# Encoder layer on eight cores: scores of an attention visit ahead of the value products of two earlier visits, a second home for folded matrices, and a new seed for the plan

## The chip, the cores and the metric

The kernel runs on the 8 cores of one Trainium2 chip (two dies of four cores). Each core computes two of the 16 sequences, with no exchange between cores. The metric is the device time of the slowest core in microseconds (us).

Some executions fall into a second, slower state, in which the cores of a die have a lower granted clock, whatever the kernel. Of the first four executions of the kernel before, two took 2221 and 2222 us and two 2437 and 2497 us.

TensorE does the matmuls, ScalarE the exponentials and many copies, VectorE sums, normalisation and many copies. In the profile's names, ps is the accumulation memory of TensorE (8 banks of 128 x 512 f32: four for scores, four for the rest). M_p holds 2 KB and 4 KB tiles, W_p bf16 weights, KV_p keys and values, S_p small bf16 tiles. wst is the weights in f32 in main memory, wsc a scratch area there for weights converted or folded once and read again.

## The reference, cut to what matters

```python
n1 = rmsnorm(h, g_mix)
q, k, v, u, gates = split(n1 @ w_in)
q, k = apply_rope(rmsnorm(q)), apply_rope(rmsnorm(k))
a = gqa_block_attention(q, k, v) @ w_attn_up       # 2048 x 2048 scores for each of 8 heads
p = (pooled(u) @ pool_w * pool_scale) @ w_pool_up
h = h + (g_a * a + g_p * p) @ w_out
# cross-attention into 256 memory tokens
xk, xv = split(rmsnorm(mem) @ w_xkv)
h = h + softmax((rmsnorm(h) @ w_xq) @ xk.T) @ xv @ w_xo
h = h + square(relu(rmsnorm(h) @ w_ff1)) @ w_ff2
return rmsnorm(h)
```

The kernel folds the cross-attention's weights with the memory tokens once per sequence (w_xq with xk into tiles A0 and A1, xv with w_xo into tiles B), 16 tiles of 4 KB for the two sequences. These are the "folded matrices". They are made in the first 230 us, beside attention 0.

## The kernel before

The work of a core is written as a list of some 6350 operations. A planner gives each an engine, a place in that engine's order, and slots for its tiles; the program then contains exactly this order, with the semaphores that it needs. A core has eight attentions (two sequences, four tiles of 512 tokens). Each has 32 visits. A visit makes four banks of scores for 256 keys and two heads, takes the exponential of all four in one instruction of ScalarE, and its value products follow one or two visits later, two visits at a time:

```python
NV, PVB = 32, 2
def visit(k):
    mms, W = [], []
    pv = range(k - PVB, k) if k >= 1 and k <= NV and k % PVB == 0 else ()
    for kk in pv:                      # value products of the two preceding visits
        P = st_["P"].pop(kk)
        ...
        mms.append(mm(..., [(Vt, kt), P], mode="c", ...))
    if k < NV:
        S = [V("S", "E") for _ in range(4)]      # the four score banks
        W.extend(S)
        ...
        mms.append(mm(..., [(K, kt // 4), q], mode="r", ...))    # scores
    if mms:
        PE(mms, W)                     # ONE operation: products first, then scores
    if k < NV:
        P = V("P", "M2")               # probabilities: a 4 KB slot
        A(exponential of ps[:, 0:4, :] into P, 2048, ...)
```

The tiles live in pools of slots. Raw weights, probabilities, running sums and gates share the ten slots of M2; bf16 weights and folded matrices share the ten slots of W:

```python
SIZES = dict(W=(10, 2048, BF16), M2=(10, 1024, F32), M1=(32, 512, F32), S1=(52, 512, BF16), KV=(4, 2048, BF16))
SEED, JITTER = 10, 60.0                # priorities are perturbed by up to 60 ns
```

After planning, `keep_warm` puts matmuls of ones by ones, whose result nobody reads, into the gaps that the plan expects in TensorE's order, where TensorE would be busy less than 80% of 3.4 us:

```python
WARM_MIN, WARM_MARGIN, WARM_SPAN, WARM_SHARE = 500.0, 450.0, 3400.0, 0.8
...
room[g[0]] = int((g[2] - g[1] - WARM_MARGIN) / FILL)      # FILL = 216 ns
```

I call these **fillers**. In the profile they are `ps<-ones_bf`. L700 is the helper's line that all matmuls have in the kernel before (L723 after), L1165 the exponential (L1197), L720 and L723 the copies and casts by ScalarE and by VectorE or GpSimd (L743, L746), L808 the logarithm of the softmax's reciprocal (L831).

The softmax here doesn't subtract the row's maximum and nothing guards it: scores larger than these inputs give would overflow.

## Time and profile before

| | value | read as |
|---|---|---|
| fast runs | 2221.2 and 2222.4 us | slow runs 2437 and 2497 are left out |
| mean span of the eight cores in the profile | 2209.3 us | less uneven than the slowest core alone; from the first to the last busy instruction, so about 5 us less than the cores view, whose mean is 2214.4 |
| attention 0, first to last exponential | 135.2 us | the stage beside the folds |
| attention 4's first to attention 7's last exponential | 937.3 us | the late stage, full of matmuls |
| fillers | 219 | 90 before 40 us, 38 in the late stage |

The stage lengths are means over the eight cores of the profile, from the starts of the 256 exponentials (32 for each attention). The prediction shows the page's lines on the engines, the stages and the waits. Two rows of the groups by form of TensorE belong beside them (columns: line, engine, operation, tiles, shapes, count, then busy us and mean ns, then idle us of TensorE just before them and what ended it):

```profile
L700 PE MATMUL ps<-S_p,KV_p 64*128 64x512 bf16 x1024 | 155.5, 382 | 6.5 <-ACT M_p L1165 5.5 <-ACT M_p L801 0.4 <-DVE M_p L1314 0.3
L700 PE MATMUL ps<-M_p,KV_p 128*64 128x512 bf16 x1024 | 137.5, 388 | 8.6 <-ACT M_p L1165 6.2 <-DVE M_p L1372 0.9 <-DVE W_p L723 0.8
```

The first row is the scores, the second the value products: together they wait 5.5 + 6.2 = 11.7 us for the exponential (L1165).

### The profile page before, as it was taken

To read this page: it belongs to the slowest core of one execution; us is meant where nothing else is said; L and a number is where in the kernel's file an instruction comes from. 1 tells how busy PE (TensorE), PEld (TensorE's weight loads), DVE (VectorE), ACT (ScalarE), POOL (GpSimd) and SP (SyncE) were. 2 spreads that over 40 slices of the span, in tenths; PEclk is the share of its full clock that TensorE was granted. 3 is DMA by queue.
4 is the path that set the end of the run, shared out by engine and by line. 5 is a ranking of instruction groups with operands and counts; after the bars stand their busy time and mean duration, and the time that the engine had idled before them with its cause. 6 is when DMAs were issued, how large, how long until landed. Compare 5 with 4: busy or idle time off the path is not lost.

```text
span 2223.7 us, 34683 instructions; the slowest of 8 cores (2205.3 to 2223.7 us)
## 1 busy us (share of the span) xinstructions
PE 2168.1 (97%) x11354; PEld 954.4 (43%) x11354; DVE 1455.3 (65%) x1793; ACT 1492.3 (67%) x1905; POOL 392.8 (18%) x286
## 2 busy tenths in 40 slices
PE   9989999999999999999999999999999999999998
PEld 5443343444444444444434443444444443444457
DVE  6877786679765687756764588457764687456403
ACT  6877778668784577844787378845786478835551
POOL 1222331223122242121120122002110112000200
PEclk9999999999999999999999999999999999999999
DMA  9977968899596973945533462436433463336353
GB/s 287 311 217 221 317 215 274 278 308 321 172 305 206 301 248 115 321 141 186 185 113 124 150 213 91 146 132 204 157 114 124 155 214 109 128 130 221 126 168 133
DMA packets 143022, 438.27 MB, mean 197 GB/s; under 512 B 16000, under 2 KB 20224, under 8 KB 142848
## 3 DMA queue, kind: packets, MB, share of 16 engines
q1 hardware_dynamic: 142848, 436.06, 60.2%
q8 instruction: 96, 1.57, 0.3%
q14 instruction: 78, 0.64, 0.1%
HBM read 372.03 MB, written 63.96 MB: 196 GB/s over the span
## 4 chain that ended last, share of the span: by engine, by line
PE 87%; DMA 5%; ACT 3%; DVE 2%; issue 2%; SPq 0%; DVEq 0%; ACTq 0%; POOL 0%; POOLq 0%
PE ps L700 87%; DMA M_p<-wst 3%; ACT M_p L1165 1%; DMA wsc<-W_p 1%; DMA outT<-M_p 1%; ACT W_p L720 0%; DVE W_p L723 0%; DMA W_p<-wsc 0%; SPq L708 0%; DVE M_p L813 0%; ACT M_p L808 0%; DMA M_p<-xT 0%; DVE M_p L1281 0%; ACT M_p L787 0%; DVE M_p L1372 0%
## 5 line engine op out<-in xcount | busy, mean ns | idle before, releaser
L700 PE MATMUL ps<-S_p,W_p 128*128 128x512 bf16 (+1 forms) x6400 | 1367.9, 369 | 10.2 <-ACT M_p L808 4.3
L700 PEld LDWEIGHTS ps<-S_p,W_p 128*128 128x128 bf16 x6400 | 611.0, 98 | 734.3 <-issue 91.3
L1165 ACT ACTIVATE M_p<-ps 128x2048 bf16<-128x2048 f32 x256 | 479.4, 1873 | 225.8 <-PE ps L700 221.0
L700 PE MATMUL ps<-M_p,W_p 128*128 128x512 bf16 (+1 forms) x1608 | 369.5, 379 | 6.6 <-ACT M_p L808 2.5
L1176 DVE TENSOR_TENSOR M_p<-M_p 128x1024 f32<-128x1024 f32 x216 | 274.8, 1272 | 148.7 <-ACT M_p L1165 144.2
L1177 DVE TENSOR_TENSOR M_p<-M_p 128x1024 f32<-128x1024 f32 x216 | 305.0, 1412 | 17.0 <-DVE M_p L1176 1.8
L796 POOL TENSOR_TENSOR M_p<-M_p 128x512 f32<-128x512 f32 x70 | 107.4, 1535 | 779.0 <-ACT M_p L787 667.5
L700 PEld LDWEIGHTS ps<-M_p,W_p 128*128 128x128 bf16 x1608 | 153.7, 98 | 203.7 <-issue 28.4
L787 ACT ACTIVATE M_p<-M_p 128x512 f32<-128x512 f32 x216 | 134.0, 624 | 118.0 <-DVE M_p L1372 45.4
L723 POOL CAST W_p<-M_p 128x1024 bf16<-128x1024 f32 x89 | 109.3, 1237 | 480.5 <-PE ps L700 303.0
L1391 ACT ACTIVATE M_p<-ps 128x512 f32<-128x512 f32 x256 | 151.9, 594 | 52.2 <-PE ps L700 50.0
L700 PE MATMUL ps<-S_p,KV_p 64*128 64x512 bf16 x1024 | 155.5, 382 | 6.5 <-ACT M_p L1165 5.5
L1395 ACT ACTIVATE S_p<-M_p 128x512 bf16<-128x512 f32 x221 | 139.2, 630 | 20.5 <-ACT M_p L1391 0.7
L700 PE MATMUL ps<-M_p,KV_p 128*64 128x512 bf16 x1024 | 137.5, 388 | 8.6 <-ACT M_p L1165 6.2
L720 ACT ACTIVATE W_p<-M_p 128x1024 bf16<-128x1024 f32 x66 | 69.0, 1050 | 96.0 <-PE ps L700 84.2
L1243 ACT ACTIVATE M_p<-ps,nbg 128x512 f32<-128x512 f32 x128 | 86.9, 684 | 53.0 <-PE ps L700 52.2
L1407 DVE TENSOR_TENSOR M_p<-ps,M_p 128x512 f32<-128x512 f32 x56 | 38.7, 691 | 118.8 <-PE ps L700 118.8
L723 DVE CAST W_p<-M_p 128x1024 bf16<-128x1024 f32 x69 | 50.4, 742 | 59.6 <-DMA M_p<-wst 23.5
L700 PEld LDWEIGHTS ps<-M_p,KV_p 128*64 128x64 bf16 x1024 | 49.6, 110 | 86.4 <-issue 62.7
L700 PEld LDWEIGHTS ps<-S_p,KV_p 64*128 64x128 bf16 x1024 | 29.6, 94 | 112.6 <-issue 112.5
L700 PE MATMUL ps<-W_p,M_p 128*128 128x384 bf16 (+1 forms) x512 | 75.3, 299 | 1.5 <-ACT W_p L720 0.9
L1394 DVE TENSOR_TENSOR S_p<-ps,M_p 128x512 bf16<-128x512 f32 x35 | 24.1, 689 | 70.8 <-ACT M_p L1391 70.6
(87 smaller groups left out, 1780.1 us busy)
## 6 DMA issues: line engine op xcount, KB each, us to landing
W_p<-wsc SPq DMA_DIRECT2D x391, 512.0 KB, 4.4
M_p<-wst SPq DMA_DIRECT2D x228, 512.0 KB, 8.7
wsc<-W_p SPq DMA_DIRECT2D x69, 512.0 KB, 8.5
M_p<-xT SPq DMA_DIRECT2D x120, 256.0 KB, 8.8
outT<-M_p SPq DMA_DIRECT2D x56, 256.0 KB, 5.7
n1d<-M_p SPq DMA_DIRECT2D x28, 256.0 KB, 6.6
M_p<-n1d SPq DMA_DIRECT2D x28, 256.0 KB, 7.2
pdd<-M_p SPq DMA_DIRECT2D x14, 256.0 KB, 7.1
```

What stands on the lines that cost most here:

```text
L700: return e.matmul(out(), lhsT=lhsT(), rhs=rhs(), start=start, stop=stop, skip_group_check=True, **kw)
L720: return e.activation(out=dst(), in_=src(), func=AF.Copy)
L723: return e.tensor_copy(out=dst(), in_=src())
L787: A(lambda e: e.activation(out=ap(sq), in_=src(), func=AF.Square), 512, False, R, [sq])
L796: TT(lambda e: e.tensor_tensor(out=ap(out), in0=ap(acc), in1=ap(sq), op=ALU.add), [acc, sq], [out])
L1165: A(lambda e: e.activation(out=b16(P).rearrange("p (a n) -> p a n", n=512), in_=ps[:, 0:4, :], func=AF.Exp, scale=0.125), 2048, True, S, [P])
L1176: D(lambda e: e.tensor_tensor(out=ap(acc), in0=ap(acc), in1=lo(), op=ALU.add), 1024, [P, acc], [acc], port=True)
L1177: D(lambda e: e.tensor_tensor(out=ap(acc), in0=ap(acc), in1=hi(), op=ALU.add), 1024, [P, acc], [acc], port=True)
L1243: A(lambda e, b=b, i=i: e.activation(out=ap(Et)[:, i * 512:(i + 1) * 512], in_=ap(b), func=AF.Exp, bias=nbg[:, i * 8 + j:i * 8 + j + 1], s ...
L1391: A(lambda e: e.activation(out=ap(rl), in_=ap(b), func=AF.Relu), 512, True, [b], [rl])
L1395: e.activation(out=ap(H), in_=ap(rl), func=AF.Square))
L1407: D(lambda e: e.tensor_tensor(out=ap(t), in0=ap(b), in1=ap(r), op=ALU.mult), 512, [b, r], [t])
```

## The change

Its intent: the exponential of an even visit shouldn't have to wait for 0.99 us of value products that stand ahead of its scores; folded matrices shouldn't have to wait for a W slot; and the plan is made again with the best seed. The core of the diff:

```diff
-SEED, JITTER = 10, 60.0
+ELSEWHERE = ("A0", "A1", "B")
+SEED, JITTER = 33, 60.0
@@ the planner's loop
+        if glued is not None:            # the products follow their visit's scores at once
+            ...
+            best = (r, "pe", glued)
@@ V(name, pool)
+            if name in ELSEWHERE:
+                v.alt = "M2"
@@ visit(k)
-                    mms, W = [], []
+                    mms, W, late = [], [], []
@@
-                        W.extend(S)
+                        smm = []
@@
-                                mms.append(mm(lambda h=h, t=t: ap(S[2 * t + h]),
+                                smm.append(mm(lambda h=h, t=t: ap(S[2 * t + h]),
@@
-                    if mms:
+                        first = PE(smm, S + W)
+                        if mms:
+                            for P in late:
+                                G.wait(first, P)      # so that the products need not wait again
+                            first.glue = PE(mms, W)
+                    elif mms:
                         PE(mms, W)
```

The planner takes an M2 slot for a folded matrix only if that is free over 300 ns earlier than a W slot.

More of the change, by code (lines that the diff above doesn't have):

```diff
@@ L45, in O2, with GROUP @@
     return ch["up"] + ch["wo"] + ch["sc"] + ch["xo"]
+def GROUP(s, tb):
+    return 2
 def AUX(query, attention, tile, blocks):
@@ L98 @@
     __slots__ = ("i", "engs", "fn", "mms", "deps", "succ", "vals", "allocs", "vt", "U", "early", "ndep", "ready", "eng",
-                 "start", "finish", "dma", "extra", "modes", "dur", "order", "place", "ps", "key", "eng_store", "port", "lead")
+                 "start", "finish", "dma", "extra", "modes", "dur", "order", "place", "ps", "key", "eng_store", "port", "lead", "glue")
 class Graph:
@@ L117, in _keys, with wait @@
             yield from self.parts.get(k, (k,))
+    def wait(self, o, v):
+        for d in self.lw[(v, 0)]:
+            if d not in o.deps:
+                d.succ.append(o)
+            o.deps[d] = 0.0
     def op(self, engs, fn, R=(), W=(), early=1e12, mms=None, dma=None, vt=None, store=False, port=False):
@@ L126, in op @@
         o.ps = False
-        o.eng_store, o.port, o.lead = store, port, 0.0
+        o.eng_store, o.port, o.lead, o.glue = store, port, 0.0, None
         reads = [(k, 0.0) for k in self._keys(R)]
@@ L292, in alloc_time @@
         return t
+    glued = None
     while n_left:
@@ L298, in schedule @@
         best = None
-        for level in range(2):
+        if glued is not None:
+            r = free_at["pe"]
+            for d, off in glued.deps.items():
+                r = max(r, d.finish + latency(d.eng, "pe") - off)
+            assert glued.ndep == 0 and all(v.slot is not None for v in glued.allocs)
+            best = (r, "pe", glued)
+        for level in range(2 if best is None else 0):
             for e in engines:
@@ L348, in schedule @@
             cand[e2].remove((o.U, o.i, o))
+        glued = o.glue
         o.eng = e
@@ L657, in ap @@
                 return ps[:, 4 + v.slot, :]
-            return tens[v.pool][:, v.slot, :]
+            t = tens[v.pool][:, v.slot, :]
+            return t.bitcast(BF16) if v.pool == "M2" and v.name in ELSEWHERE else t
         def halves(name, n):
@@ L1097, in attention_steps @@
             K, Vt = kv_tiles(s)
-            NV, PVB = 32, 2
+            NV, PVB = 32, GROUP(s, tb)
             def visit(k):
                 def f():
-                    mms, W = [], []
+                    mms, W, late = [], [], []
                     finish = []
@@ L1107, in f @@
                         P = st_["P"].pop(kk)
+                        late.append(P)
                         if v == 0:
@@ L1129, in f @@
                             ac = st_["accb"][c]
+                            late.append(ac)
                             parts.append((lambda h, ac=ac: b16(ac)[:, h * 512:h * 512 + 512], ac))
@@ L1142, in f @@
                         ac = st_["accb"][c]
+                        late.append(ac)
                         for h in range(2):
```

## The prediction

> **What bounds the kernel now.** I read the page's busy table first, then the cores, then the windows by stage, and inside the one stage with idle TensorE the waits, the chain and the timeline.
>
> ```profile
> PE 2168.1 (97%) x11354; PEld 954.4 (43%) x11354; DVE 1455.3 (65%) x1793; ACT 1492.3 (67%) x1905; POOL 392.8 (18%) x286
> ```
> ```profile
> core 1: 2223.7 us, clock 0.996
> core 2: 2205.3 us, clock 0.998
> ```
> ```profile
> core 1: us, PE busy (x) PEld busy (x) DVE busy (x) ACT busy (x) POOL busy (x), PEclk, DMA share, GB/s
> ...
> 92.00:232.00 140.00, 120.86 (x685) 49.63 (x685) 103.68 (x116) 107.65 (x108) 26.74 (x22) 0.96 0.79 240
> 232.00:400.00 168.00, 164.78 (x817) 66.77 (x818) 126.28 (x149) 138.00 (x175) 48.19 (x36) 0.99 0.83 267
> 400.00:2212.00 1812.00, 1793.71 (x9278) 785.80 (x9277) 1155.03 (x1393) 1178.52 (x1488) 297.12 (x206) 1.00 0.55 183
> ```
>
> TensorE is busy 97% of the span, so only its idle time and its useless work can go. After 400 us it idles 1812 - 1793.7 = 18.3 us in 1812. The one weak stage is 92 to 232 us: 19.1 us idle of 140 and a granted clock of 0.96. That stage holds the folds of the memory matrices with the attention of block 0 beside them. Core 2 runs the same program, had a clock of 1.00 there, and is 18.4 us shorter: the slowest core is slow because of this stage.
>
> From the steps between starts of consecutive matmuls in the trace of core 1 I split its span: 2084 us of streaming, 63 us of array-mode switches (660 steps that are 95 ns longer, 311 ns where the usual step is 216), 66 us of waits (5 of them lost to the half clock), and about 10 us before the first and after the last matmul. The streaming includes 219 matmuls of ones by ones that the plan itself puts into expected gaps to keep the clock up: 219 x 0.216 = 47 us, 109 - 30 = 79 of them before 30 us, where nothing else can run. So 66 + 47 = 113 us is all that any plan could win with the same arithmetic, and some 20 us of it is the unavoidable start.
>
> What TensorE waits for in the weak stage (us in total, times, longest):
>
> ```profile
> PE ps L700 <- ACT M_p L1165: 7.2, 9, 1.6
> PE ps L700 <- ACT M_p L808: 4.3, 1, 4.3
> PE ps L700 <- DVE W_p L723: 3.7, 6, 1.1
> PE ps L700 <- ACT W_p L720: 2.8, 1, 2.8
> ```
>
> L1165 is the softmax exponential. The tile view of wsc and the chain, both from the weak stage, show who is behind the others:
>
> ```profile
>   ACT W_p L720: 10.5, 3
>   DVE W_p L723: 9.0, 2
> ```
> ```profile
> 156.19 8.00 DMA wsc<-W_p
> ...
> 217.56 14.38 DMA wsc<-W_p
> ```
>
> Evictions of folded matrices into W slots (L720, L723) sit 10.5 and 9.0 us waiting for a store of an earlier folded matrix to leave its slot, and those stores are 22.4 us of the chain of 140. The 4.3 us wait at 166 us comes right after the first of them.
>
> **What the skill says, and the trace.** "PSUM — Partial Sum Buffer", Terms: two engines on one bank at once is an error. The four score banks are all read by one exponential, so the next scores must wait for its end; in the trace scores start 0.14 us after it, never before. "ScalarE: Activation LUTs", What ACT_TABLE_LOAD costs: 186 ns plus 0.833 ns per element, 1.89 us for 2048; the trace has 1.873, so the exponential is at its floor and can only start sooner. "TensorEngine Tiling (Array Packing)", Key Properties: changing the tiling mode drains the array; the trace shows 95 ns per change. "TensorE: Matmul & The Clock Gate", What's actually happening: an idle window of about 3.4 us halves the clock; here the 12 matmuls of 256 columns after the 4.26 us gap took 2.53 us where twelve others took 1.48.
>
> **Part 1, scores first.** The loop of block 0 where nothing else fills it (start, us, what):
>
> ```profile
> 144.42 1.05 PE L700 MATMUL ps<-M_p,KV_p 128*64 128x512 bf16 x8 [0.76 <-ACT M_p L1165]
> 145.41 0.61 PE L700 MATMUL ps<-S_p,KV_p 64*128 64x512 bf16 x4
> 145.94 1.48 PE L700 MATMUL ps<-S_p,W_p 128*128 128x256 bf16 x12
> 148.19 0.61 PE L700 MATMUL ps<-S_p,KV_p 64*128 64x512 bf16 x4 [0.76 <-ACT M_p L1165]
> ```
> ```profile
> 146.17 1.88 ACT L1165 ACTIVATE M_p<-ps 128x2048 bf16<-128x2048 f32 x1 [0.42 <-PE ps L700]
> 148.95 1.88 ACT L1165 ACTIVATE M_p<-ps 128x2048 bf16<-128x2048 f32 x1
> ```
>
> Every second visit has the value products of two visits (144.42 to 145.41, 0.99 us) ahead of its scores. Scores to exponential is 0.76 us, the exponential 1.88, back to TensorE 0.14. An odd visit takes 0.76 + 1.88 + 0.14 = 2.78 us, which is 148.19 - 145.41; an even one 3.77; a pair 6.55. Afterwards both take 2.78, a pair 5.56. Over the 16 pairs of a block that is 15.8 us less chain, 127 us over all eight blocks. But the chain counts only where TensorE runs out of other work. The matmuls are the same and the mode changes too: full, column, row, full was three changes, full, row, column, full is three. The added waits of the scores (for the probabilities and the sum of earlier visits) are on things done one or more visits before. So what TensorE can win is its wait for L1165: 7.2 us in the stage and 11.7 us in the whole run. I take two thirds of the first and half of the other 4.5: 5 + 2 = **7 us**. The 221 us that ScalarE waits for scores win nothing themselves; ScalarE is at 67%.
>
> **Part 2, folded matrices in 4 KB slots of the other pool.** Same transfers, same evictions; 16 tiles (A0 and A1 of four heads, then eight B) get 10 more slots to choose from. It removes the two long slot waits: 4.3 + 2.8 us plus a later 1.35 us at 232.82 that the timeline marks with the same releaser, 8.4 us, and with them the half clock: 0.04 x 140 = 5.6 us. The 3.7 us behind L723 I take for casts of raw weights, which stay. Against it, the other pool holds raw weights, probabilities and gates, and the DMA is at 0.79 of its time here and 0.96 from 200 to 300 us, so part comes back as a wait for weights. I take 6 of 8.4 and 4 of 5.6: **10 us**.
>
> **Part 3, seed of the plan.** It perturbs priorities by up to 60 ns, adds no instruction, but moves every choice after the first. Some of the 140 fillers after 30 us (30 us of time) and of the 18.3 us late idle can go either way. A seed is surely picked as the best of several, but so was the one before: **3 us**, with some 8 us either way.
>
> Sum: 7 + 10 + 3 = 20 us, so 2222.4 - 20 = **2202 us**. It agrees with a second estimate from before alone: core 2, which escaped most of the half clock, is at 2205.
>
> **Rivals.** (A) Nothing moves. TensorE is full after 400 us, and in the stage the wait for the exponential becomes one for weights, as the DMA share of 0.96 from 200 to 300 us suggests. Against it: 92 to 232 us is at 0.79. Time: 2216 to 2225. (B) The other pool becomes the bound: folded matrices wait for a store of 9 us there, raw loads and probabilities find no slot, and TensorE waits on casts. The queue's waits for slots freed by the casts speak for it, 84 us in the stage by ACT, DVE and POOL; the choice of the slot that is free first speaks against. Time: 2225 to 2245. (C) The seed carries it all, as the plan is remade and the weak stage is so uneven: anywhere from 2195 to 2225, with the gain not in the stage. (D) Everything in the stage closes and the late gaps too: 25 us + half of 18.3 + 5 of fillers, about 39 us, 2183.
>
> **Range and chances.** D gives the low end and A the high end: **2184 to 2218 us**. Over 2% faster means under 2178, more than every loss in the stage and half of the rest: 0.06. Over 2% slower needs 2267, beyond B: 0.01. Within 2%: 0.93.
>
> **What would show each step.** Part 1: scores directly ahead of value products at even visits, exponentials of block 0 spaced 2.8 us in starved stretches, TensorE's wait for L1165 down from 11.7 to about 5 us, the switch count near 660. Part 2: no eviction waiting 5 us for a wsc store, folded matrices named M_p as outputs, clock 0.98 or more in the stage on core 1, its idle from 19 to under 9 us. Part 3: ones-by-ones matmuls near 219, and idle after 400 us near 18 us. I am wrong if the gain lies after 400 us, if the weak stage keeps its idle under another releaser (DMA of raw weights), or if all cores slow evenly.

## The result, and the profile after

The kernel after took 2217.0 us (median of four fast runs, 2213.8 to 2220.0) against 2221.2 and 2222.4: about 5 us less, where 20 were forecast. The ratio is 0.9978, 95% interval 0.9954 to 1.0003. Ratios here are the mean time of one kernel's fast runs over that of the other's in the same rounds, so not quite the ratio of the quoted medians. Executions in which one die ran at a lower clock are left out of the means.

The page of after, its slowest and its fastest core, and the windows by stage:

```profile
span 2215.8 us, 34632 instructions; the slowest of 8 cores (2200.1 to 2215.8 us)
PE 2160.2 (97%) x11331; PEld 949.3 (43%) x11331; DVE 1444.3 (65%) x1798; ACT 1488.6 (67%) x1904; POOL 393.1 (18%) x282
```
```profile
core 0: 2200.1 us, clock 0.999
...
core 4: 2215.8 us, clock 0.997
```
```profile
core 4: us, PE busy (x) PEld busy (x) DVE busy (x) ACT busy (x) POOL busy (x), PEclk, DMA share, GB/s
...
92.00:232.00 140.00, 123.84 (x714) 49.97 (x713) 108.96 (x119) 113.96 (x118) 33.89 (x24) 0.98 0.79 243
...
400.00:2212.00 1812.00, 1783.73 (x9225) 780.07 (x9223) 1143.40 (x1406) 1169.85 (x1483) 285.94 (x195) 1.00 0.54 183
```

There are 23 instructions of TensorE fewer (11354 to 11331), all fillers (219 to 196). The weak stage of 92 to 232 us has an idle time of 16.2 us where it had 19.1, and clock 0.98 where it had 0.96, each on its slowest core (means over the six cores with a complete record: 14.4 and 16.3 us idle). After 400 us the idle time went *up* from 18.3 to 1812 - 1783.7 = 28.3 us, while busy time fell by 10.

The waits of TensorE in the weak stage (us, times, longest) and the groups of scores and of value products:

```profile
PE ps L723 <- DVE W_p L746: 6.1, 9, 1.7
PE ps L723 <- ACT M_p L1197: 6.1, 10, 1.9
PE ps L723 <- DVE M_p L746: 1.9, 1, 1.9
PE ps L723 <- DVE S_p L1218: 1.5, 1, 1.5
```
```profile
L723 PE MATMUL ps<-S_p,KV_p 64*128 64x512 bf16 x1024 | 155.4, 381 | 17.7 <-ACT M_p L1197 14.0 <-DVE M_p L746 1.9 <-DVE M_p L1439 0.4
L723 PE MATMUL ps<-M_p,KV_p 128*64 128x512 bf16 x1024 | 137.1, 388 | 0.3 <-ACT M_p L1197 0.3
```

The wait for the exponential did not fall. It moved from the value products, which now hardly ever wait (0.3 us), to the scores. In the waits of the whole run, before and after:

```profile
PE ps L700 <- ACT M_p L1165: 11.7, 19, 1.6
```
```profile
PE ps L723 <- ACT M_p L1197: 14.3, 24, 1.9
```

The order itself is as meant. The timeline in the weak stage, TensorE and then ScalarE (start, us, what):

```profile
201.90 0.61 PE L723 MATMUL ps<-S_p,KV_p 64*128 64x512 bf16 x4
202.44 1.05 PE L723 MATMUL ps<-M_p,KV_p 128*64 128x512 bf16 x8
...
208.57 0.61 PE L723 MATMUL ps<-S_p,KV_p 64*128 64x512 bf16 x4 [1.18 <-ACT M_p L1197]
```
```profile
206.56 1.87 ACT L1197 ACTIVATE M_p<-ps 128x2048 bf16<-128x2048 f32 x1
...
209.33 1.88 ACT L1197 ACTIVATE M_p<-ps 128x2048 bf16<-128x2048 f32 x1
```

Scores (64x512) stand ahead of products (128x512), and where nothing else comes between, exponentials are 209.33 - 206.56 = 2.77 us apart, as worked out. Attention 0 is 11 us shorter. The next table has means over the eight cores of a profile; "again" is a second run of the kernel after on another chip (e7 below).

| stage, us | before | after | again |
|---|---|---|---|
| attention 0, first to last exponential | 135.2 | 124.2 | 124.6 |
| start of attention 1 | 257.2 | 253.6 | 252.5 |
| attention 1 to attention 2 | 258.7 | 263.1 | 261.6 |
| attention 2 to attention 4 | 550.0 | 550.0 | 550.1 |
| attention 4 to the end of attention 7 | 937.3 | 931.1 | 931.1 |
| from there to the end | 206.1 | 206.5 | 206.5 |
| mean span | 2209.3 | 2204.2 | 2201.8 |

Of 11 us won in attention 0, 4 to 5 are left at the start of attention 1, and none or two at the start of attention 2. Then 6.2 us come in the stage that looked full.

A ledger of TensorE's **lost time** makes this plainer: everything in the steps from one matmul's start to the next that is neither streaming nor a mode switch, and the fillers whole. It is worked out from the trace, as in the prediction, over the cores with a complete record of matmuls (six of eight).

| lost us, by time | before | after | again |
|---|---|---|---|
| 0 to 92 | 26.7 | 27.9 | 26.8 |
| 92 to 400 | 30.5 | 26.5 | 23.7 |
| 400 to 520 | 7.9 | 11.4 | 12.6 |
| 520 to 1066 | 16.6 | 19.4 | 15.0 |
| 1066 to 2000 | 14.9 | 8.7 | 8.7 |
| 2000 to 2190 | 7.0 | 7.3 | 7.4 |
| sum | 103.6 | 101.2 | 94.2 |

So there are three things to explain: a gain from 92 to 400 us of 4 to 7 us where parts 1 and 2 had forecast 17; a loss of 4 us from 400 to 520 us; and a late gain of 6 us that the prediction had not.

The tile view of wsc from 92 to 300 us shows what became of the slots. Of before, all three lines on who waited (the prediction shows the last two), then of after:

```profile
  POOL W_p L723: 20.5, 2
  ACT W_p L720: 10.5, 3
  DVE W_p L723: 9.0, 2
```
```profile
L735 SPq DMA_DIRECT2D wsc<-M_p x2: 320/323/326, 166.2 to 232.7; - x2
...
  POOL W_p L746: 20.3, 3
  DVE W_p L746: 1.6, 1
```

The waits of 10.5 us (ScalarE) and 9.0 us (VectorE) for a store are gone or down to 1.6. GpSimd's wait of 20 us was there before and stays. Only 2 of the 16 folded matrices were stored from an M2 slot.

### The profile page after: what moved, and what is told of

Its sections match the earlier page's. It is cut to its first block, busy times and chain, and to the rows that moved or that the text cites. A ratio compares the mean times of both kernels' runs of the same rounds, so it can differ in the third digit from the quotient of the medians.

```text
span 2215.8 us, 34632 instructions; the slowest of 8 cores (2200.1 to 2215.8 us)
## 1 busy us (share of the span) xinstructions
PE 2160.2 (97%) x11331; PEld 949.3 (43%) x11331; DVE 1444.3 (65%) x1798; ACT 1488.6 (67%) x1904; POOL 393.1 (18%) x282
## 4 chain that ended last, share of the span: by engine, by line
PE 83%; DMA 7%; ACT 4%; DVE 2%; issue 2%; SPq 1%; POOL 0%; DVEq 0%; ACTq 0%; POOLq 0%
PE ps L723 83%; DMA M_p<-wst 4%; DMA wsc<-W_p 2%; ACT M_p L1197 2%; SPq L731 1%; DVE M_p L836 1%; DMA outT<-M_p 1%; ACT W_p L743 1%; ACT M_p L1423 0%; DMA wsc<-M_p 0%; DVE W_p L746 0%; ACT M_p L831 0%; DVE M_p L1208 0%; DVE M_p L1497 0%; POOL W_p L746 0%
## 5 line engine op out<-in xcount | busy, mean ns | idle before, releaser
L1208 DVE TENSOR_TENSOR M_p<-M_p 128x1024 f32<-128x1024 f32 x216 | 271.4, 1257 | 155.3 <-ACT M_p L1197 152.7
L1209 DVE TENSOR_TENSOR M_p<-M_p 128x1024 f32<-128x1024 f32 x216 | 296.0, 1370 | 14.4
L819 POOL TENSOR_TENSOR M_p<-M_p 128x512 f32<-128x512 f32 x73 | 114.7, 1572 | 855.3 <-ACT M_p L810 850.0
L810 ACT ACTIVATE M_p<-M_p 128x512 f32<-128x512 f32 x216 | 133.7, 624 | 101.2 <-DVE M_p L1404 51.6
L746 POOL CAST W_p<-M_p 128x1024 bf16<-128x1024 f32 x92 | 118.0, 1289 | 410.1 <-DMA M_p<-wst 186.1
L743 ACT ACTIVATE W_p<-M_p 128x1024 bf16<-128x1024 f32 x66 | 69.1, 1051 | 103.6 <-PE ps L723 78.9
L746 DVE CAST W_p<-M_p 128x1024 bf16<-128x1024 f32 x66 | 47.1, 734 | 59.2 <-DMA M_p<-wst 25.3
L1426 DVE TENSOR_TENSOR S_p<-ps,M_p 128x512 bf16<-128x512 f32 x39 | 26.8, 688 | 67.9 <-ACT M_p L1423 67.6
```

Source lines behind the costliest of these rows:

```text
L743: return e.activation(out=dst(), in_=src(), func=AF.Copy)
L746: return e.tensor_copy(out=dst(), in_=src())
L810: A(lambda e: e.activation(out=ap(sq), in_=src(), func=AF.Square), 512, False, R, [sq])
L819: TT(lambda e: e.tensor_tensor(out=ap(out), in0=ap(acc), in1=ap(sq), op=ALU.add), [acc, sq], [out])
L1208: D(lambda e: e.tensor_tensor(out=ap(acc), in0=ap(acc), in1=lo(), op=ALU.add), 1024, [P, acc], [acc], port=True)
L1209: D(lambda e: e.tensor_tensor(out=ap(acc), in0=ap(acc), in1=hi(), op=ALU.add), 1024, [P, acc], [acc], port=True)
```

## The experiments

Eighteen kernels ran. "Late stage" is attention 4 to the end of attention 7.

### First round: which part?

All four, and the kernel before beside them, had a second die with a clock near 0.97 or lower. I use the mean over the cores of die 0 in the executions in which its clock was 0.98 or more (four of 46 are left out), with its standard error; the kernel before had **2232.8 ± 1.2 us**. Die 0 was not undisturbed either: in the four profiles its clock records stand at 0.8125 for 98 to 151 us, and fast executions of the kernel before on other chips have a mean of 2213 to 2215 us. So these numbers count only among themselves.

**e1: scores first under the old plan.** The plan of the kernel before is made as it was, and every operation that holds both parts is then cut in two, with scores ahead; slots, engines and fillers stay. The edit in outline (its helper of some 30 lines is left out):

```diff
+order = transplant(plan made with whole visits, seed 10)
+# each operation with both parts: first = scores, then glued products
-ELSEWHERE = ("A0", "A1", "B")
+ELSEWHERE = ()
```

> The plan of the kernel before (seed 10, every instruction of every engine in its place, 219 filler matmuls), in which only each even visit is cut in two so that its four score matmuls stand ahead of its value products. Theory W (until about 520 us the stream of raw weights sets the pace, and after that TensorE is full): block 0's attention may end up to 10 us earlier than the mean of 227.0 us over the cores, but the start of block 2's attention stays within 2 us of 515.9, and the ratio to before is 0.999 to 1.000. Rival R (the swap itself makes the gain of the change): ratio 0.996 to 0.998, TensorE's wait for the exponential halves from 11.7 us.

Measured: 2230.6 ± 1.7 us, 2 us less than before and within the errors; late stage 937.9 us, so unchanged. Attention 0 took 133.4 us, so the 10 us that it might have gained did not come.

**e2: seed 33 in the kernel before.**

```diff
-SEED, JITTER = 10, 60.0
+SEED, JITTER = 33, 60.0
```

> The kernel before with the seed 33 in place of 10 and nothing else. Rival S (the gain of 0.0022 is the luck of the seed): ratio 0.996 to 0.999. Theory W with a seed that was picked for other rules: ratio 1.001 to 1.005, that is 2 to 11 us slower.

Measured: 2240.7 ± 1.0 us, 8 us *more*. Late stage 939.7.

**e3: scores first with the old seed, without the slots.**

```diff
-ELSEWHERE = ("A0", "A1", "B")
-SEED, JITTER = 33, 60.0
+ELSEWHERE = ()
+SEED, JITTER = 10, 60.0
```

> Scores first with the glued value products, planned anew, but with the old seed 10 and without the other pool's slots. Rival R: ratio 0.996 to 0.998 whatever the seed. Theory W: 0.998 to 1.003, as the gain before 330 us is lost again by 520 us; the seed then decides on which side of 1 it lies.

Measured: 2236.0 ± 1.2 us, 3 more than before, but the late stage took 933.0 us.

**e4: everything but the seed.**

```diff
-SEED, JITTER = 33, 60.0
+SEED, JITTER = 10, 60.0
```

> The whole change but for the seed, which stays 10. If the slots in the other pool matter, it differs from the run with scores first alone by over 3 us; if they do not (only two of sixteen folded matrices took such a slot in the changed kernel, by its two stores out of M_p), it is the same within 2 us.

Measured: 2235.6 ± 0.6 us, late stage 933.7.

What follows: e3 and e4 differ by the slots alone, and by 0.4 ± 1.3 us: no effect of the slots shows with seed 10 (with seed 33 they were never taken out alone). Seed 33 is a bad one for the old order (e2, 8 us), and 10 not a good one for the new (e4); both are seen on this chip alone. The late gain is there with scores first *and* a remade plan (e3, e4), and not with either the order alone (e1) or the seed alone (e2). The same holds of attention 0: 126.7 and 126.6 us in e3 and e4 over all cores, and 133.1 on die 0 of e2.

### Second round: the late gain

**e5: the kernel before without its late fillers.** Fillers that the plan has between 1040 and 2030 us are left out.

```diff
-        if i in at:
+        if i in at and not 1.04e6 < at[i][1] < 2.03e6:
```

> The kernel before, plan and order kept, with the filler matmuls that the plan puts between 1040 and 2030 us left out (some 38 of the 219). Theory F (in the full part the wait for the exponential is not an idle TensorE but a gap that the plan foresees and fills with ones-by-ones matmuls): the fillers stand beside a wait, so leaving them out gives nothing: fourth to last block within 2 us of before, TensorE's idle time up by some 38 x 0.216 = 8 us, most of it released by the exponential. Rival G (the fillers themselves lengthen the path): 6 to 8 us faster.

**e6: the same edit on e1** (scores first under the old plan).

> The kernel before's plan with the scores of even visits moved ahead of their value products, and the same late fillers left out. Theory F: now the exponential starts 1 us earlier and the gap can close: the stretch from block 4's first exponential to block 7's last one becomes 4 to 7 us shorter than in the kernel before and in the run that only leaves the fillers out. Rival (late gain comes from the new plan's order alone): no shorter than before.

Measured: e5 2221.6 us, ratio 0.9988 (0.9949 to 1.0027); e6 2220.0 us, ratio 0.9986 (0.9946 to 1.0025). Late stage 937.9 and 937.6 us, so e6 missed its forecast of 4 to 7 us less. (By the mean over the dies outside the slow state e6 is 2 to 3 us below the kernel before, 2211.9 ± 0.5 against 2214.5 ± 0.7; neither the late stage nor attention 0, 133.6 us against 134.0 in e5, has it.) Taking 38 x 0.216 = 8.2 us of useless matmuls out of TensorE's stream did not shorten the stage: they stand beside waits. The timeline shows which. The kernel before, at one place of attention 6:

```profile
1613.01 0.61 PE L700 MATMUL ps<-S_p,KV_p 64*128 64x512 bf16 x4
1613.54 2.76 PE L700 MATMUL ps<-ones_bf 128*128 128x512 bf16 x12
1616.24 1.05 PE L700 MATMUL ps<-M_p,KV_p 128*64 128x512 bf16 x8
```

e5, the same place (its profile is of another core, some 5 us earlier):

```profile
1607.76 0.61 PE L700 MATMUL ps<-S_p,KV_p 64*128 64x512 bf16 x4
1610.98 1.05 PE L700 MATMUL ps<-M_p,KV_p 128*64 128x512 bf16 x8 [2.61 <-ACT M_p L808]
```

And the kernel after, at its like place:

```profile
1604.57 0.61 PE L723 MATMUL ps<-S_p,KV_p 64*128 64x512 bf16 x4
1605.11 1.05 PE L723 MATMUL ps<-M_p,KV_p 128*64 128x512 bf16 x8
```

Before, TensorE had after these scores nothing but the products of the visit just scored and the one before it. It had to wait for that visit's exponential and a logarithm behind it, 2.6 us; twelve fillers stood there, so the profile called it busy. After, the products that follow are of the two earlier visits, and there is no wait. The waits of TensorE from 1066 to 2005 us, of e5 and of after:

```profile
PE ps L700 <- ACT M_p L808: 5.7, 7, 2.6
PE ps L700 <- DVE M_p L1372: 3.8, 4, 0.9
...
PE ps L700 <- ACT M_p L1165: 0.5, 2, 0.3
```
```profile
PE ps L723 <- ACT M_p L831: 4.1, 8, 0.7
```

Without fillers the old order shows 11.8 us of late waits, and only 0.5 of them by the name of the exponential, against the expectation (a wait for several semaphores bears the name of the last; the logarithm stands behind the exponential in ScalarE's order). With scores first the plan has 4.1 us and 8 fillers (1.7 us). The fillers of that stage, before and after:

```profile
L700 PE MATMUL ps<-ones_bf 128*128 128x512 bf16 x38 | 9.7, 379 | 0.0
```
```profile
L723 PE MATMUL ps<-ones_bf 128*128 128x512 bf16 x8 | 2.4, 379 | 0.0
```

30 fillers fewer are 30 x 0.216 = 6.5 us; the stage is 6.2 us shorter. That cutting the operations under the old plan (e6) recovers none of it shows that the gain needs the *planner*. That it orders other work differently once a visit needs no such gap is how I read the timelines above; no run tests it by itself.

**e7: the kernel after again**, unedited, on this chip.

> The changed kernel itself beside the kernel before on this chip, so that the others have it as a yardstick: ratio 0.995 to 1.000, about 5 us faster, with the stretch from block 4 to 7 shorter by 6 us (30 fillers fewer x 0.216 = 6.5 us).

Measured: 2216.6 us (three fast, one slow), ratio 0.9973 (0.9932 to 1.0013); late stage 931.1 again. The mean over the dies outside the slow state is 2207.9 ± 0.9 against 2215.1 ± 0.9 for before: 7 us.

**e8: the slots alone.** The lines of `ELSEWHERE` in the kernel before.

```diff
+ELSEWHERE = ("A0", "A1", "B")
...
+            if name in ELSEWHERE:
+                v.alt = "M2"
```

> The kernel before, seed 10, with only the other pool's slots allowed to folded matrices. Two of sixteen matrices take one. If that is worth something it shows before 260 us; expectation of theory W: within 3 us of the kernel before either way, from the remade plan, and the long waits of evictions for a store of an earlier folded matrix do not all go.

Measured: 2222.7 us, ratio 0.9993 (0.9954 to 1.0031), attention 0 133.2 us, late stage 937.3. No gain of the second home shows by itself, as with e3 and e4; two matrices took it here too.

### Third round: where the early lead goes

**e9 and e10: half the bytes of each raw weight**, in the kernel before and after. The cast reads the loaded half twice, so the result is wrong (relative error 0.98); order and slots are the same.

```diff
-load(lambda r=r: ap(r), wst[uid, hf], 524288, [r])
+load(lambda r=r: ap(r)[:, 0:512], wst[uid, hf][:, 0:512], 524288, [r])
```

> The kernel before with the same plan, instructions and waits, but each raw-weight load brings only its first 512 columns, which the cast then reads twice: half the bytes of that stream, a wrong result on purpose. Theory W (the raw-weight stream sets the pace until about 520 us): TensorE's idle time before block 4 falls from 36 us to under 22 us and the attention of block 2 starts 10 us or more earlier than 516 us. Rival P (the plan's own order and its fillers set the pace there, the transfers are hidden): under 4 us earlier.

> The same halving in the changed kernel. Theory W: the lead of 6 us that the changed kernel has where block 0's feed-forward starts is no longer lost, so the attention of block 2 starts 4 to 8 us earlier than in the halved kernel before. Rival P: it starts at the same time or later (14 more fillers between the starts of blocks 1 and 3 are worth 3 us), as it did with whole loads (516.7 against 515.9 us).

Measured: e9 2225.9 us (two runs 20 us apart, ratio 1.0007 with a wide interval of 0.9943 to 1.0072); e10 had one fast run, 2207.6 us, and one slow. Attention 1 to 2 took 259.7 us in e9 and 261.9 in e10, so part of the difference between the two orders (2.2 us of 3 to 4) stays with half the traffic. The sign was another one, the start of attention 2. Over all eight cores it reads 517.9 us in e9 and 511.8 in e10, 6 us earlier, which would speak for the traffic. But die 0 of e9's profile was disturbed (two of its cores at clock 0.983). By its other die attention 1 starts at 253.5 us and attention 2 at 513.3; e10 has 249.9 and 511.8. So of a lead of 3.6 us, 1.5 are left at attention 2 with half the bytes, where 0 to 2 of 4 to 5 were left with all of them. Traffic alone is not what eats the lead. Half the bytes also brings attention 2 some 3 us earlier under both orders. This is one profile of each kernel.

**e11 and e12: an eleventh slot in M2**, in the kernel after. e11 has seed 32; e12 has seed 76 and no bias against the other pool.

```diff
-M2=(10, 1024, F32)
+M2=(11, 1024, F32)
-SEED, JITTER = 33, 60.0
+SEED, JITTER = 32, 60.0         # e12: 76, and ALT_BIAS = 0.0
```

> The changed kernel with eleven instead of ten slots in the 4 KB pool of raw weights, probabilities and gates, and seed 32, picked for that. If the raw loads wait for slots more than for bandwidth, the stretch before block 4 shortens by 3 to 8 us against the changed kernel, and the late stretch stays at 931 us: ratio to before 0.993 to 0.996. If only bandwidth counts: same as the changed kernel, 0.9975.

> As the run before, with seed 76 and without the planner's penalty of 300 ns on taking a slot in the other pool, so that more folded matrices should go there. If those slots are worth something when they are used, the first 260 us shorten by 3 us or more against the changed kernel; else it is within 2 us of the run with seed 32.

Measured: e11 **2213.1 us, ratio 0.9948 (0.9930 to 0.9966)**, correct, and the first interval clear of 1. Attention 1 to 2 fell to 257.4 us. e12 2217.6 us (three fast, two slow), ratio 0.9963 (0.9937 to 0.9990), attention 1 to 2 256.8, late stage 933.6 with 13 fillers. Dropping the bias too brought nothing more (three of the 16 matrices were stored from M2). It is the slot, or the seed, which these two runs do not separate.

### Fourth round: fillers, seed or slots?

**e13: the kernel after without the 43 fillers between 260 and 530 us.**

```diff
-        if i in at:
+        if i in at and not 2.6e5 < at[i][1] < 5.3e5:
```

> The kernel after with the same plan, but the 43 matmuls of ones that stand between the starts of attention 1 and attention 3 (260 to 530 us) left out; correct. Theory F, these matmuls cost their time: attention 1 to attention 2 falls from 263 us by up to 7 us, towards 256, and the end with it, 2210. Theory G, they stand in waits which are there without them: attention 1 to 2 stays at 262 to 264 us, TensorE's idle time there grows by about the 7 us of the matmuls left out, and the end stays at 2215 to 2219.

Measured: 2221.4 us (three fast, one slow), ratio 0.9998 (0.9981 to 1.0015). The stage became *longer*, 265.5 us. Its window of 400 to 520 us (columns as in the windows above), and the longest of TensorE's waits from 300 to 600 us in it:

```profile
400.00:520.00 120.00, 108.83 (x512) 45.27 (x513) 82.90 (x108) 65.13 (x78) 29.28 (x24) 0.96 0.94 282
```
```profile
PE ps L723 <- ACT M_p L1197: 7.5, 4, 3.1
```

In the kernel after, TensorE's wait for the exponential in these 300 us is 1.8 us, so the fillers stood in waits here too. They also earned something: without them the clock is 0.96, and the ledger has 9.7 us lost to half clock in the whole run, where the kernel after lost some 4 and again 1.8. Theory F falls.

**e14: the kernel after with seed 24; e15: the kernel before with seed 7.**

```diff
-SEED, JITTER = 33, 60.0
+SEED, JITTER = 24, 60.0         # e15: 10 becomes 7, in the kernel before
```

> The kernel after with seed 24 in place of 33: its plan has 41 matmuls of ones between attention 1 and 2 and none between 2 and 3, 190 in all against 196, 8 late. Late gain from the rule (scores first): from attention 4 to the end of attention 7 takes 931 to 933 us as with seeds 33, 10 and 32. Late gain from the seed: it goes back towards 937. The early part, if it follows the seed: attention 1 to 2 differs from 263 us by more than 3 us. Total 2212 to 2226.

> The kernel before with seed 7 in place of 10: its plan has 27 late matmuls of ones against 38, 44 between attention 1 and 3 against 29. Late gain from the rule: from attention 4 to the end of attention 7 stays at 936 to 940 us. If it went by the number of late matmuls of ones alone: 11 x 0.216 = 2.4 us less, 934.9. The early part, if the seed of the kernel before was a lucky one: attention 4 starts later than in the kernel before by 3 to 8 us, total 2224 to 2232.

Measured: e14 2225.3 us, ratio 1.0017 (0.9999 to 1.0035), late stage **930.9**. Attention 1 starts at 258.8 us, 5 later than with seed 33; attention 1 to 2 takes 264.2 us, so the early part differs, but not where it was expected to. e15 2224.4 us (middle of the three fast runs; three slow), ratio 1.0015 (0.9990 to 1.0040), late stage **935.9** with 27 fillers.

The late stage of every plan, by rule:

| | late stage, us (late fillers) |
|---|---|
| products first | before 937.3 (38), e2 939.7 (37, slow chip), e15 935.9 (27), e16 936.3 (28), e17 937.3 (38) |
| scores first, plan remade | after 931.1 (8), e3 933.0 and e4 933.7 (8, slow chip), e12 933.6 (13), e14 930.9 (8), e11 and e18 930.9 (8) |

The rule carries the late gain, with five seeds; a luckier seed under the old rule gets 1 of the 6 us. Attention 0 goes by the same rule: 131 to 135 us with products first, 123 to 127 with scores first and the plan remade, and 133.6 in e6, whose order alone was changed. But a seed decides what is left of it: with seed 24 the changed kernel is no faster than the one before.

**e16: the kernel before with eleven slots** (seed 15, one of the best two of 40 in the plan's own time).

```diff
-M2=(10, 1024, F32)
+M2=(11, 1024, F32)
-SEED, JITTER = 10, 60.0
+SEED, JITTER = 15, 60.0
```

> The kernel before with an eleventh 4 KB slot and seed 15 (among the two best of 40 in the plan's own time), to see whether the gain of that slot needs the change. If the slot's gain and that of the scores add up: the early part as short as with the eleventh slot in the kernel after (attention 1 to 2 in 257 us), the late part at 936 to 940, total about 2217 to 2222. If it needs the scores first: no gain, 2222 to 2228.

Measured: 2222.3 us (three fast, one slow), ratio 1.0005 (0.9982 to 1.0028); attention 1 to 2 258.1 us, late stage 936.3. No gain of the eleventh slot shows for the old order; as the seed was changed with it, the one could hide the other.

**e17: the kernel before with nine slots; e18: the kernel after with eleven and its own seed.**

```diff
-M2=(10, 1024, F32)
+M2=(9, 1024, F32)               # e18: 11, in the kernel after
```

> The kernel before with nine 4 KB slots in place of ten, same seed 10: how much the early stage hangs on the number of slots, the other suspect for the lost lead, since with the scores first a probability tile is held longer (1.65 slots on average against 1.44 in attention 0, 1.45 against 1.30 from attention 2 to 4, counted in the plan). Theory P, slots pace the raw loads: attention 1 to 2 grows from 258.7 us to 265 or more, attention 4 starts 8 to 14 us later, total 2230 to 2237; then a tenth to a fifth of a slot is worth 1 to 3 us, part of the lost lead. Theory Q, slots do not pace it: attention 4 starts within 3 us of the kernel before.

> The kernel after with an eleventh 4 KB slot and its own seed 33, so that the slot is the one difference (the earlier run with eleven changed the seed too). Theory P: attention 1 to 2 falls from 262 to 263 us to 256 to 259, the lead at attention 2 is kept, total 2210 to 2214. Theory Q, the gain of the earlier run was its seed: attention 1 to 2 stays above 260, total 2215 to 2222.

Measured: e17 2238.3 us in the four fast runs (two slow), ratio 1.0075 (1.0055 to 1.0094). Attention 1 to 2 grew to 265.2 us, attention 4 starts 15.1 us later, and from there on the core is on time: all of the loss is made while raw weights come in (the last load starts at 972 us). e18's fast runs took **2211.2 and 2211.5 us, ratio 0.9955 (0.9931 to 0.9978)**; attention 1 to 2 took 258.1 us, mean span 2199.3. Part of that shorter stage is a later start: attention 1 starts at 255.6 us here (257.2 in e11 and e12), where after and again have 253.6 and 252.5, so that attention 2 starts at 513.6 us against 516.7 and 514.1. The window of 400 to 520 us in before, after, e17 and e18:

```profile
400.00:520.00 120.00, 117.53 (x575) 49.11 (x574) 90.10 (x108) 79.18 (x98) 33.96 (x25) 1.00 0.91 294
```
```profile
400.00:520.00 120.00, 114.48 (x554) 48.13 (x553) 82.45 (x111) 68.23 (x84) 31.05 (x24) 1.00 0.93 293
```
```profile
400.00:520.00 120.00, 113.98 (x555) 47.69 (x552) 81.77 (x100) 72.62 (x88) 29.54 (x24) 1.00 0.88 286
```
```profile
400.00:520.00 120.00, 115.90 (x563) 48.18 (x561) 89.77 (x111) 79.32 (x94) 38.07 (x27) 1.00 0.94 305
```

With a slot too few, ScalarE and VectorE do less in this window (79 and 90 us become 73 and 82), and TensorE has less to do; that less raw weight is there to be cast is my reading. The kernel after looks like the kernel before with a slot less; with a slot more it looks like the kernel before. The means over eight cores say so for ScalarE: 79.0 us before, 71.4 and 73.2 in after and again, 74.8 in e17, 78.1 to 79.2 with eleven slots.

Why would the new order need a slot more? Scores first means that the exponential writes its probabilities while those of the two earlier visits are still being read. From the starts of exponentials and the ends of their value products in the traces, a probability tile is held 8.17 us on average in attention 1 before and 9.71 after, and 9.32 and 11.18 in attentions 2 and 3. That is 1.01 and 1.18 of the ten slots in attention 1, and 1.08 and 1.30 in attentions 2 and 3: about 0.2 slot more. If a whole slot is worth e17's 15 us, 0.2 of one is an estimated 3 us. The ledger from 400 to 520 us fits: 7.9 us lost before, 11.4 to 14.6 in the five runs with scores first, a remade plan and ten slots (after, e7, e10, e13, e14), 8.2 to 10.0 in the three with eleven (e11, e12, e18).

Three things keep this from being shown. In the same ledger e17, with a whole slot less, loses only 1.6 us more than before in these 120 us, and most of its loss (10.8 us) from 520 to 1066 us, where after and again lose 3 more and 2 less. e15, with products first, ten slots and another seed, loses 3.1 us more here without any longer holding. And no run shortened the holding alone. So that the number of slots paces the early stage is shown by e17; that the longer holding is what eats the lead is a fit of numbers, and the plan's other choices remain a rival. The eleventh slot's own gain is not clear of the noise either: by the mean over the cores and the fast runs, against the kernel before on the same chip, again is 7.9 ± 1.2 us shorter, e11 9.9 ± 0.9, e12 9.6 ± 0.9 and e18 7.7 ± 0.7.

## Why the prediction was wrong

It forecast 2202 us; the kernel took 2217. The time was inside the range, a hair under its upper end (2218, though the rival that was to set this end went on to 2225), and the chance of 0.93 for "within 2%" was right. The gain was not. Most of what is missing is part 2.

**Part 1, 7 us forecast.** The chain was read rightly: the order, the 2.78 us between exponentials, the time of the mode switches (62.7 and 62.4 us). But the shorter chain gives attention 0 nothing by itself: with the plan kept, it stayed at 133.6 us (e6), and it fell to 124 only where the planner made a new plan round it. The step that failed is "So what TensorE can win is its wait for L1165: 7.2 us in the stage and 11.7 us in the whole run". It failed twice. In and about the weak stage, attention 0 became 11 us shorter, but TensorE won 4 to 7 us from 92 to 400 us, and its wait for the exponential is 14.3 us where 11.7 was: the exponentials come earlier, and TensorE meets the same waits elsewhere. ScalarE's wait for scores is 221 us as before. In the late stage, the wait that could be won had no L1165 to its name: it was covered by fillers and, with these taken out, named for the logarithm (e5). I had the number of fillers, 219, and wrote of those after the start only, under the seed, that some "can go either way". They were the map of the waits: 38 late fillers said 8.2 us of gaps in a stage whose idle time I read as full. "I am wrong if the gain lies after 400 us" is what came true. That the 7 us of this part lie near the whole gain of 5 to 6 us is luck: 6 of them came in a stage that it had ruled out.

**Part 2, 10 us forecast.** The step that failed is the win: "It removes the two long slot waits: 4.3 + 2.8 us plus a later 1.35 us", "and with them the half clock". The waits of ScalarE and VectorE for a store did go in the kernel after (10.5 and 9.0 us to 0 and 1.6), TensorE's waits of 4.3 and 2.8 us are gone from the stage's list, and the clock rose to 0.98 as forecast. But TensorE's idle time fell by 3 us and not by 10, because other waits took their place: 6.1 us for VectorE's copies into W (L746), which had been 3.7, and 1.9 and 1.5 us for two more operations of VectorE. Nor is it the slots that do much to the waits for a store: the planner used 2 of them for 16 tiles, and e8, with the same two, still has 3.4 to 5.2 us of ScalarE and 3.9 to 5.7 of VectorE on the cores of die 0. e3, without the slots, has 2.7 to 4.0 of ScalarE. e8 and the pair of e3 and e4 measure the part: no gain, within about 1 us. Why the planner took only two is not shown; that M2 is itself short fits (e17: one slot is worth 15 us). The rival that spoke of the other pool as the bound may be right about the pool, but it looked to the folded matrices there; the probabilities are what stay longer.

**Part 3, 3 us with 8 either way.** The spread was about right: e2 is 8 us worse (on the disturbed chip) and, against seed 33, e14 some 7 to 9 us (an estimate across chips). As each kernel has its own chosen seed, the two choices about cancel; no run separates a rest of 3 us.

**The rivals.** Rival A named the time, 2216 to 2225, and the place in part: the lead is lost where raw weights come in. But with half their bytes most of it is lost too (e10 against e9's undisturbed die), so it is not their traffic alone. Rival C said that the gain would not be in the stage and that the seed carries it. The late gain is not in the stage, but it is the rule's, with five seeds; what is left of the early one is the seed's (e14). The number of fillers (forecast near 219, found 196) and the idle time after 400 us (forecast near 18, found 28) had been named as signs, and both spoke against my account.

**What was missing.** The sum had no term for what the new order costs: it called the added waits harmless, "on things done one or more visits before", which is so, and did not ask how much longer a tile is held. About 4 us are lost between 400 and 520 us; that the longer holding is their cause is not shown, and it stays open.

The sum by the ledger, the mean of after and again against before: +0.6 up to 92 us, -5.4 up to 400, +4.1 up to 520, +0.6 up to 1066, -6.2 in the late stage, +0.4 to the end: -5.9 us. The mean spans say -6.3, the median of the slowest core -5.4.

One line of the prediction's sums is garbled: 79 fillers do stand before 30 us, but "109 - 30" has no source. And its tile view of wsc left out GpSimd's 20.5 us, the longest of the three.

The second estimate, "core 2, which escaped most of the half clock, is at 2205", misled: it described what one core can have by luck. After, too, the cores spread from 2200 to 2216 us.

The experiments gave a kernel that is clear of the one before, though within 2%: the change with eleven slots, 2211 to 2213 us at ratios 0.9948 (e11) and 0.9955 (e18). That it beats the kernel after is not shown: the intervals overlap with 0.9954 to 1.0003 and 0.9932 to 1.0013.

## What to carry to other kernels

Where a plan fills expected gaps with dummy work, count that work by stage before believing that a stage is full, and take it out once to see the names of the waits beneath. An order that starts a consumer's input earlier also holds its buffers longer: the added holding time, times what one slot is worth in a run with one slot less, gives a first estimate of the cost, to be tested. Move an order under the old plan before crediting it with a gain: here that gave none in the two stages that the new plan shortened. And compare planned kernels over several seeds, as one seed can move as much as such a change does.

## What the Trainium skill lacked or had wrong

- "TensorE: Matmul & The Clock Gate", Seeing it yourself: it tells one to budget a clock of 13/16 once three cores of a die run dense matmuls. The fast runs here don't show it: all eight cores run matmuls 97% of the time at a mean granted clock of 0.995 to 0.999, with 216 ns for 512 columns, and no clock record of a profile of before or after stands at 13/16. The disturbed profiles do show that clock, 0.8125, but for a part of the span: 319 to 395 us on the cores of die 1 in the first round, 98 to 151 us on die 0. So a dense kernel on all cores met this clock in some executions and not in others; what decides it is not shown.
  On the half clock: without 43 fillers, 9.7 us are lost to half clock instead of 1.8 to some 4, and the mean over the cores is about 3 us longer than with them (e13 against after and e7, on other chips).
- "TensorEngine Tiling (Array Packing)", Key Properties, says that a change of mode drains the array and gives no duration. The trace has 95 ns for each of 660 changes, 63 us of 2222.
- No page says how dummy matmuls mislead a profile: in the kernel before, 38 of them hid waits of some 8 us in a stage that read as full, and taking them out left the time as it was (ratio 0.9988).
